# A decoder layer whose inputs are laid out by the host: one DMA for a token tile, contiguous weight tiles

## The chip, the cores and the metric

The kernel runs on one core of a Trainium2 chip. The time is that of the device for one launch, in microseconds (us). Rearranging arrays on the host before and after the launch is not in it. Before the change three runs gave 2838.21, 2841.0 and 2851.06 us, so the median is 2841.0 us.

The engines are PE (TensorE, matrix products), DVE (VectorE), ACT (ScalarE), POOL (GpSimd) and SP (SyncE). In this kernel SP issues every DMA, one after the other, and the 16 DMA engines of the core carry them out.

## The reference

One decoder layer on 2048 tokens of 1024 numbers, all in float32:

```python
h  = rmsnorm(x, g_mix)
zb, zc, zx, zq, zk, zv = split(h @ w_in)          # 6 x 512 columns
y_c = zb * causal_dwconv3(zc * zx, conv_w, conv_b)
y_a = dilated_attention(rmsnorm(zq), rmsnorm(zk), zv)   # 8 heads, 3 branches: dilation 1, 4, 16
x  = x + concat(rmsnorm(y_c, g_out_conv), rmsnorm(y_a, g_out_attn)) @ w_out
h  = rmsnorm(x, g_ffn)
x  = x + (silu(causal_dwconv3(h @ w_gate, ...)) * (h @ w_up)) @ w_down      # 2816 wide
x  = x + sigmoid(rmsnorm(x, g_ple) @ w_ple_gate) * (p @ w_ple_proj)
```

## The kernel before

A float32 product is made of three matmuls: each operand is split into a high and a low half (`split`, L91 and L92: ACT rounds, POOL or DVE subtracts), and `mm3` (L95) adds high x high, high x low and low x high. With an operand 512 wide one such matmul is the unit of PE's work here.

The 2048 tokens are four chunks `c` of 512. In a chunk the tokens are reordered, so that the dilated branches read plain slices: the token 16a + b of a chunk (a below 32, b below 16) stands at 32b + a. A tile of 128 rows therefore holds four values of b, with 32 tokens each. In the array x these 32 tokens lie 16 rows apart. `tokens` (L65 to L69) loads or stores such a tile as four DMAs of 32 partitions, one for each b. It is used for x at the start (tile `xt`), for x again in the first residual (tile `t` of `project`), for p in the last stage, and for the result.

The program has three parts in a row. `qkv` normalizes and transposes x, multiplies with the q, k and v columns of w_in and spills the results to DRAM. `mix` runs the attention and, paced beside it, the convolution group, whose weights come as tiles `craw` (L286). `rest` runs a list of stages: three `project` stages (w_out and the residual), `gate_up` and `down` for two halves of the tokens, and `ple`. Products of 2 x 2 blocks are made with seven block products instead of eight.

In `project` (its name stands in `rest`), chunks 0 and 1 are treated together, first the convolution's part of w_out in two halves of 512 columns. For each half and each chunk, a loop over four k blocks loads y (`load_y`, L823, tile `s`), splits it to a tile `g` on ACT (L828) and DVE (L829), and runs 12 matmuls on it. After a chunk DVE adds the result to x (L906, tile `t`), and the sum is stored to `xd` (L908). Tiles `s` and `g` have four buffers each, tiles `t` eight.

The order of the instructions on each engine is not that of the code. The framework's scheduler puts them in order with a model of their durations; then each engine, and SP's queue of DMAs too, runs in that fixed order. An instruction that waits holds up all behind it on its engine. The DMAs take turns on eight completion semaphores, and a DMA whose turn comes waits until the DMA eight places before it has landed, as the wait lists of the built program have it.

Of the kernel before, what the change touches and what calls it, by code (L numbers as in the profile page):

```python
# [19 lines left out]
P = 128  # L20
SEQ = 2048
D = 1024
DFF = 2816
PLE = 256
CW = 512
NH = 8
HD = 64
KD = D // P
# [11 lines left out]
class Layer:  # L40


    def __init__(self, tc, a, out, ctx):
        self.tc, self.nc, self.a, self.out, self.ctx = tc, tc.nc, a, out, ctx
        nc = self.nc
        self.const = ctx.enter_context(tc.tile_pool(reuse_waits="tile", name="const", bufs=1))
        self.dram = ctx.enter_context(tc.tile_pool(name="dram", bufs=1, space=DRAM))
        self.ident = self.const.tile([P, P], F32, name="ident")
        make_identity(nc, self.ident)
        d = self.dram  # L50
        self.hd = [d.tile([KD, P, QT], F32, name=f"hd{c}") for c in range(NQ)]
        self.qd = [d.tile([2, 2, HD, SEQ], F32, name=f"qd{p}") for p in range(4)]
        self.kd = [d.tile([2, 2, HD, SEQ], F32, name=f"kd{p}") for p in range(4)]
        self.vd = [d.tile([QT, NH, 2 * HD], F32, name=f"vd{c}") for c in range(NQ)]
        self.ycd = [d.tile([P, SEQ], F32, name=f"ycd{i}") for i in range(4)]
        self.yad = [d.tile([P, SEQ], F32, name=f"yad{i}") for i in range(4)]
        self.xd = [[[d.tile([P, D], F32, name=f"xd{i}{c}{j}") for j in range(4)] for c in range(NQ)] for i in range(3)]
        self.gd = [d.tile([7, NF // 2, P, QT], F32, name=f"gd{h}") for h in range(2)]
        self.bd = [[d.tile([P, D], F32, name=f"bd{i}{j}") for j in range(4)] for i in range(2)]
        self.td = [d.tile([NF // 2, P, 2, 512], F32, name=f"td{i}") for i in range(2)]  # L60
        self.xq = a["x"].rearrange("(c a b) m -> c b a m", a=32, b=16)
        self.pq = a["p"].rearrange("(c a b) m -> c b a m", a=32, b=16)
        self.oq = out.rearrange("(c a b) m -> c b a m", a=32, b=16)

    def tokens(self, tile, dram, c, j, store=False):  # L65

        for b in range(4):
            rows, part = dram[c, 4 * j + b], tile[32 * b:32 * b + 32]
            self.nc.sync.dma_start(*((rows, part) if store else (part, rows)))  # L69

    def rsqrt(self, pool, ss, n, scale):

# [56 lines left out]
    def qkv(self):  # L129
        nc, tc, a = self.nc, self.tc, self.a  # L130
        with ExitStack() as st:
# [11 lines left out]
            gq = wvp.tile([P, 4], F32, name="gq")  # L143

            def gains():
                for i in range(2):
                    nc.sync.dma_start(gk[64 * i:64 * i + 64], a["k_norm_g"].rearrange("(d o) -> d o", o=1))
                    nc.sync.dma_start(gq0[64 * i:64 * i + 64], a["q_norm_g"].rearrange("(d o) -> d o", o=1))
                for p in range(4):
                    for i in range(2):  # L150
                        s = slice(64 * i, 64 * i + 64)
                        nc.vector.tensor_scalar(gq[s, p:p + 1], gq0[s], 2.0 ** (2 * p + i - 2), None, ALU.mult)

            whl = {w: [(wvp if w == 2 else wp).tile([P, KD, 512], F32R, name=f"w{w}{s}") for s in "hl"] for w in range(3)}
            wv = a["w_in"].rearrange("(k p) n -> p k n", p=P)

            def load_w(w):
                for k in range(0, KD, 2):
                    raw = stage.tile([P, 2, 512], F32, name="raw", tag="raw")
                    c0 = 3 * CW + 512 * w  # L160
                    nc.sync.dma_start(raw, wv[:, k:k + 2, c0:c0 + 512])
                    self.split(whl[w][0][:, k:k + 2], whl[w][1][:, k:k + 2], raw, nc.gpsimd if w or k % 4 else nc.vector)

            def load_x(c, j):
# [114 lines left out]

    def load_conv_w(self, n):  # L280
        nc, pool = self.nc, self.cwp
        c0 = CW * (1, 2, 0)[n % 3] + P * (n // 3 % 4)
        halves = []
        for k in range(0, KD, 4):
            raw = pool.tile([P, 4, P], F32, name="craw", tag="craw", bufs=4)
            nc.sync.dma_start(raw, self.a["w_in"].rearrange("(k p) n -> p k n", p=P)[:, k:k + 4, c0:c0 + P])  # L286
            hi = pool.tile([P, 4, P], F32R, name="chi", tag="chi", bufs=5)
            lo = pool.tile([P, 4, P], F32R, name="clo", tag="clo", bufs=5)
            (nc.scalar.copy if k else nc.vector.tensor_copy)(hi, raw)  # L289
            nc.gpsimd.tensor_tensor(lo, raw, hi.bitcast(F32), ALU.subtract)  # L290
            halves.append((hi, lo))
        return [(hi[:, k], lo[:, k]) for hi, lo in halves for k in range(4)]

    def conv(self):

        nc, a, st = self.nc, self.a, self.cst
        cp = st.enter_context(self.tc.tile_pool(reuse_waits="tile", side="right", name="cp", bufs=1))
        work = st.enter_context(self.tc.tile_pool(reuse_waits="tile", side="right", name="cwork", bufs=1))
        cw = cp.tile([P, 4, 3], F32, name="cw")
        cb = cp.tile([P, 4], F32, name="cb")  # L300
        for i in range(3):
            nc.sync.dma_start(cw[:, :, i], a["conv_w"][i].rearrange("(k p) -> p k", p=P))
        nc.sync.dma_start(cb, a["conv_b"].rearrange("(k p) -> p k", p=P))
        carry = cp.tile([P, 4, 2, 2, 1], F32, name="carry")
        yield
        cols = [(c, i, z) for c in range(NQ) for i in range(4) for z in (1, 2, 0)]
        w, hq = self.conv_w, self.conv_h
        for n, (c, i, z) in enumerate(cols):
            if n and i == 0 and z == 1:
                hq = self.load_conv_h(c)  # L310
            ps = self.cpm.tile([P, QT], F32, name="zps", tag="zps")
            for k in range(KD):
                m = self.mm3(ps, *w[k], hq[k][:, 0], hq[k][:, 1], k == 0, k == KD - 1)
                if k % 2 == 0:
                    self.pace(m, 4 * n + k // 2)
            if n + 1 < len(cols):
                w = self.load_conv_w(n + 1)
            if z == 1:
# [12 lines left out]
            yield  # L331
# [260 lines left out]
    def weight_units(self, stages):  # L592
# [4 lines left out]
        for name, *arg in stages:  # L597
# [5 lines left out]
            elif name == "gate_up":  # L603
                for f in range(NF // 2):
                    for w in (a["w_gate"], a["w_up"]):
                        yield w.rearrange("(k p) n -> p k n", p=P)[:, :, 2 * f * P:2 * f * P + 2 * P]
            elif name == "down":
                b = a["w_down"].rearrange("(f i p) (s n) -> i s p f n", i=2, p=P, n=512)
                t = [t.rearrange("f p s n -> s p f n") for t in self.td]
                for m in (b[0, 0], t[1][1], b[1, 0], t[0][1], t[0][0], t[1][0], b[1, 1]):  # L610
                    for f in range(0, NF // 2, 2):
                        yield m[:, f:min(f + 2, NF // 2)]
# [40 lines left out]
    def rest(self):  # L653
# [3 lines left out]
        with ExitStack() as st:  # L657
# [16 lines left out]
            row = lambda tag: (rows if tag == "t" else sums if tag == "c" else small).tile([P, 512], F32, name=tag, tag=tag)  # L674
            operand = lambda tag="w": (big if tag == "w" else late).tile([P, 2, 512], F32R, name=tag, tag=tag)
            go = cp.tile([P, 2, 4], F32, name="go")
            for i, n in enumerate(("g_out_conv", "g_out_attn")):
                nc.sync.dma_start(go[:, i], a[n].rearrange("(k p) -> p k", p=P))
            cw = cp.tile([P, NF, 3], F32, name="fcw")
            cb = cp.tile([P, NF], F32, name="fcb")  # L680
            for i in range(3):
                nc.sync.dma_start(cw[:, :, i], a["ffn_conv_w"][i].rearrange("(k p) -> p k", p=P))
            nc.sync.dma_start(cb, a["ffn_conv_b"].rearrange("(k p) -> p k", p=P))
            carry = cp.tile([P, NF, 2, 1], F32, name="fcarry")
            ones = cp.tile([P, 1], F32, name="ones")
            nc.vector.memset(ones, 1.0)
# [496 lines left out]
    return r  # L1183


def build(shapes):
    nc = bacc.Bacc("TRN2", target_bir_lowering=False, num_devices=1, dynamic_dma_scratch_size=1024)
    a = {n: nc.dram_tensor(f"in_{n}_dram", s, F32, kind="ExternalInput").ap() for n, s in shapes.items()}
# [19 lines left out]
```

## Time and profile before

| | us |
|---|---|
| median of three runs | 2841.0 |
| the profiled execution | 2845.52 |
| its span, first to last instruction | 2843.8 |
| PE busy in the span | 2638.9 |
| DVE busy | 1908.9 |
| POOL busy | 1520.2 |
| ACT busy | 1320.3 |

The 16 DMA engines moved 467.66 MB of the kernel's data and were busy for 53.2% of the span. PE is busy for 93% of the span, so what is to be gained lies in the stretches in which PE waits. They are found in the table of busy time by 40 us, and the reason in the list of waits and in the order of events on each engine. The trace's mean clock of PE is 0.977 of the full one; the table names the clock for each stretch.

### The profile page before, as it was taken

The page shows a single profiled execution, that of the slowest core. Times are in us where ns is not written, and L with a number is a line of the kernel's source. Part 1 is how long each engine was busy: PE and PEld are TensorE (multiplying, and loading weights), DVE is VectorE, ACT ScalarE, POOL GpSimd, SP SyncE. Part 2 cuts the span into 40 slices and gives each one's busy share as a digit, 9 for nine tenths or more (in the row PEclk, how much of TensorE's full clock was granted, in tenths as well). Part 3 has the DMA queues.
Part 4 walks back from the last instruction along what each step waited for, and adds up shares of the span by engine and source line. Part 5 has one row for each costly group of instructions (what it writes and reads, how often), then busy time and mean ns, then how long its engine had stood idle before and what let it go on. Part 6 is the DMA issues. An engine that isn't in the chain of part 4 may idle for free. (4 is left out here: it accounts for less than half of the span.)

```text
span 2843.8 us, 38213 instructions
## 1 busy us (share of the span) xinstructions
PE 2638.9 (93%) x12320; PEld 2174.1 (76%) x12320; DVE 1908.9 (67%) x3355; ACT 1320.3 (46%) x2941; POOL 1520.2 (53%) x1050
## 2 busy tenths in 40 slices
PE   6999989999899869899889999999999999998998
PEld 5777778888788658677677787877878777786787
DVE  8776656767676555987767778457677776647543
ACT  3322257767768234453334444444444445444332
POOL 4111311624343724478786678575666668767554
PEclk9999989999899989999999999999999999999999
DMA  6444566675755778665552236673323326665343
GB/s 185 149 136 124 174 151 152 182 173 148 196 154 152 213 222 306 195 224 205 199 193 97 97 125 213 232 240 106 101 102 104 112 89 212 222 227 195 97 124 88
DMA packets 374473, 470.10 MB, mean 165 GB/s; under 512 B 51072, under 2 KB 214528, under 8 KB 374272
## 3 DMA queue, kind: packets, MB, share of 16 engines
q1 hardware_dynamic: 374272, 467.66, 53.2%
q8 instruction: 97, 1.59, 0.2%
q14 instruction: 104, 0.85, 0.1%
HBM read 339.53 MB, written 127.99 MB: 164 GB/s over the span
## 5 line engine op out<-in xcount | busy, mean ns | idle before, releaser
L95 PE MATMUL ps<-t,w 128*128 128x512 f32 x4368 | 1034.4, 396 | 45.9 <-DVE u L757 23.1
L95 PEld LDWEIGHTS ps<-t,w 128*128 128x128 f32 x4368 | 819.8, 189 | 247.2 <-DVE u L757 28.7
L92 POOL TENSOR_TENSOR w<-raw,w 128x512 fp32r<-128x512 f32 x318 | 477.3, 1510 | 298.4 <-ACT w L91 281.9
L92 POOL TENSOR_TENSOR w<-s,w 128x512 fp32r<-128x512 f32 x208 | 298.8, 1441 | 178.4 <-ACT w L91 172.4
L95 PE MATMUL ps<-w,g 128*128 128x512 f32 x1368 | 342.6, 399 | 52.9 <-ACT g L828 22.3
L95 PEld LDWEIGHTS ps<-w,g 128*128 128x128 f32 x1368 | 258.2, 191 | 118.8 <-ACT g L828 24.9
L290 POOL TENSOR_TENSOR clo<-craw,chi 128x512 fp32r<-128x512 f32 x96 | 125.8, 1317 | 394.7 <-ACT chi L289 132.1
L95 PE MATMUL zps<-hq,chi 128*128 128x512 f32 x768 | 257.1, 412 | 9.2 <-DVE yc L329 5.9
L91 ACT CAST w<-raw 128x512 fp32r<-128x512 f32 x318 | 192.5, 615 | 94.1 <-PE ps L95 90.8
L91 ACT CAST w<-s 128x512 fp32r<-128x512 f32 x208 | 127.9, 617 | 228.3 <-PE ps L95 196.2
L95 PE MATMUL ps<-w,t 128*128 128x512 f32 x852 | 212.1, 395 | 6.8 <-POOL w L92 4.7
L440 ACT ACTIVATE pt<-so,md 128x256 f32<-128x256 f32 (+1 forms) x384 | 174.9, 457 | 84.5 <-DVE md L437 82.6
L95 PEld LDWEIGHTS ps<-w,t 128*128 128x128 f32 x852 | 160.8, 190 | 44.8 <-POOL w L92 7.3
L437 DVE CUSTOM_DVE_ANT_0 so<-s,neg 128x256 f32<-128x256 f32 (+1 forms) x384 | 130.3, 362 | 64.8 <-PE s L434 53.1
L706 DVE TENSOR_TENSOR s<-raw 128x512 f32<-128x512 f32 x88 | 113.4, 1289 | 83.4 <-POOL w L92 82.5
L95 PEld LDWEIGHTS zps<-hq,chi 128*128 128x128 f32 x768 | 142.1, 196 | 35.2 <-DVE yc L329 7.2
L92 DVE TENSOR_TENSOR g<-g 128x512 fp32r<-128x512 f32 x84 | 97.2, 1162 | 98.2 <-ACT g L91 93.2
L95 PE MATMUL zps<-hq,clo 128*128 128x512 f32 x384 | 154.5, 403 | 0.0
L433 PE MATMUL s<-kk,qs 128*128 128x256 f32 (+1 forms) x384 | 132.9, 353 | 20.6 <-DMA kk<-kd 18.2
L434 PE MATMUL s<-kk,qs 128*128 128x256 f32 (+1 forms) x384 | 137.1, 361 | 14.8 <-DMA v<-vd 5.8
L174 POOL TENSOR_TENSOR raw<-hT 128x1024 f32<-128x1024 f32 x16 | 39.0, 2438 | 202.4 <-DVE rs_h L78 187.5
L473 DVE TENSOR_TENSOR nb<-po,nb 64x512 f32<-64x512 f32 x96 | 92.1, 959 | 63.9 <-ACT nb L472 62.9
(214 smaller groups left out, 5118.4 us busy)
## 6 DMA issues: line engine op xcount, KB each, us to landing
gd<-t SPq DMA_DIRECT2D x110, 256.0 KB, 2.0
craw<-in_w_in_dram SPq DMA_DIRECT2D x96, 256.0 KB, 4.0
raw<-in_w_gate_dram SPq DMA_DIRECT2D x44, 512.0 KB, 3.7
raw<-in_w_up_dram SPq DMA_DIRECT2D x44, 512.0 KB, 3.5
g<-gd SPq DMA_DIRECT2D x84, 256.0 KB, 4.3
raw<-td SPq DMA_DIRECT2D x40, 512.0 KB, 4.0
t<-gd SPq DMA_DIRECT2D x70, 256.0 KB, 4.3
v<-vd SPq DMA_DIRECT2D x264, 64.0 KB, 2.6
```

Source lines behind the costliest of these rows:

```text
L91: self.nc.scalar.copy(hi, src)
L92: lo_engine.tensor_tensor(lo, src, hi.bitcast(F32), ALU.subtract)
L95: mm = lambda *a, **k: self.nc.tensor.matmul(*a, **k, **kw)
L174: nc.gpsimd.tensor_tensor(t, hT[:, :, 0].bitcast(F32), hT[:, :, 1].bitcast(F32), ALU.add)
L290: nc.gpsimd.tensor_tensor(lo, raw, hi.bitcast(F32), ALU.subtract)
L433: mm(s[:, lo:], qb[l], cols[0], start=True, stop=False)
L434: mm(s[:, lo:], qb[l], cols[1], start=False, stop=True)
L437: nc.vector.tensor_tensor_reduce(out=so[:, lo:], in0=s[:, lo:], in1=neg[:, br, lo:], scale=-slope, scalar=3.0e38, op0=ALU.add, op1=ALU.min ...
L440: nc.scalar.activation(pt[:, l, lo:], so[:, lo:], AF.Exp, bias=md[:, 0, col:col + 1], scale=-1.0, accum_out=md[:, 1, col:col + 1])
L473: nc.vector.tensor_tensor(dst, like(po[other], br), dst, ALU.add)
L706: nc.vector.tensor_tensor(t, x, y, op)
```

## The change

The host now rearranges the inputs before the launch, and the result after it (`lay_out`, and the last line of `kernel`); it computes nothing. x, p and the result stand in the kernel's order of tokens, so a tile of 128 tokens is one DMA of 128 partitions. The columns of w_in for the convolution are cut into 12 tiles of 128 columns, those for q, k and v into three of 512, w_gate and w_up into tiles of 256 columns, each with the partition first, so that what a partition receives is contiguous. Filters, biases and gains are stored by partition as well, and each is one DMA.

```diff
-        self.xq = a["x"].rearrange("(c a b) m -> c b a m", a=32, b=16)
-        self.pq = a["p"].rearrange("(c a b) m -> c b a m", a=32, b=16)
-        self.oq = out.rearrange("(c a b) m -> c b a m", a=32, b=16)
+        self.xq, self.pq, self.oq = [t.rearrange("(c j r) m -> c j r m", c=NQ, r=P) for t in (a["x"], a["p"], out)]
 
     def tokens(self, tile, dram, c, j, store=False):
-        for b in range(4):
-            rows, part = dram[c, 4 * j + b], tile[32 * b:32 * b + 32]
-            self.nc.sync.dma_start(*((rows, part) if store else (part, rows)))
+        self.nc.sync.dma_start(*((dram[c, j], tile) if store else (tile, dram[c, j])))
...
-                for i in range(2):
-                    nc.sync.dma_start(gk[64 * i:64 * i + 64], a["k_norm_g"].rearrange("(d o) -> d o", o=1))
-                    nc.sync.dma_start(gq0[64 * i:64 * i + 64], a["q_norm_g"].rearrange("(d o) -> d o", o=1))
+                nc.sync.dma_start(gk, a["k_norm_g"])
+                nc.sync.dma_start(gq0, a["q_norm_g"])
...
-                    nc.sync.dma_start(raw, wv[:, k:k + 2, c0:c0 + 512])
+                    nc.sync.dma_start(raw, a["w_qkv"][w, :, k:k + 2])
...
-            nc.sync.dma_start(raw, self.a["w_in"].rearrange("(k p) n -> p k n", p=P)[:, k:k + 4, c0:c0 + P])
+            nc.sync.dma_start(raw, self.a["w_conv"][z, :, k:k + 4])
...
-        for i in range(3):
-            nc.sync.dma_start(cw[:, :, i], a["conv_w"][i].rearrange("(k p) -> p k", p=P))
-        nc.sync.dma_start(cb, a["conv_b"].rearrange("(k p) -> p k", p=P))
+        nc.sync.dma_start(cw, a["conv_w"])
+        nc.sync.dma_start(cb, a["conv_b"])
...
-                        yield w.rearrange("(k p) n -> p k n", p=P)[:, :, 2 * f * P:2 * f * P + 2 * P]
+                        yield w[f]
...
-            for i, n in enumerate(("g_out_conv", "g_out_attn")):
-                nc.sync.dma_start(go[:, i], a[n].rearrange("(k p) -> p k", p=P))
+            nc.sync.dma_start(go, a["g_out"])
...
+def lay_out(a):
+    by = lambda t, shape, *axes: np.ascontiguousarray(t.reshape(shape).transpose(axes))
+    tokens = lambda t: by(t, (NQ, 32, 16, -1), 0, 2, 1, 3).reshape(SEQ, -1)
+    w_in, g_out = a.pop("w_in"), np.stack([a.pop("g_out_conv"), a.pop("g_out_attn")])
+    return dict(
+        a, x=tokens(a["x"]), p=tokens(a["p"]), g_out=by(g_out, (2, 4, P), 2, 0, 1),
+        w_conv=by(w_in[:, :3 * CW], (KD, P, 12, P), 2, 1, 0, 3), w_qkv=by(w_in[:, 3 * CW:], (KD, P, 3, 512), 2, 1, 0, 3),
...
```

The scheduler gives the changed program another order in four places: the first tiles of x, the first loads of the convolution's weights, the `project` stages, and the stores of `ple`. Everywhere else each engine has the same order as before.

On SP, at the end of `mix` and the beginning of the first `project`, the order was this (`s` is the tile of y for a k block, `ycd` and `yad` the stored y of the two groups, `xd` the stored residual):

```order
L823 DMA s<-ycd_84 128x512
L330 DMA ycd_84<-yc 128x512
L69 DMA t<-in_x_dram 32x512 x18
L908 DMA xd_89<-t 128x512
L908 DMA xd_90<-t 128x512
L908 DMA xd_91<-t 128x512
L69 DMA t<-in_x_dram 32x512
L908 DMA xd_92<-t 128x512
L69 DMA t<-in_x_dram 32x512 x13
```

It goes on with four `e<-yad`, the stores `xd_93` to `xd_96` with three pieces of `t` between them, and 13 further pieces; only then comes the next `s<-ycd_81`. Now the same place reads:

```order
L813 DMA s<-ycd_84 128x512
L322 DMA ycd_84<-yc 128x512
L65 DMA t<-in_x_dram 128x512 x8
L813 DMA e<-yad_85 128x512
L813 DMA e<-yad_86 128x512
L813 DMA e<-yad_87 128x512
L813 DMA e<-yad_88 128x512
L813 DMA s<-ycd_81 128x512
L813 DMA s<-ycd_82 128x512
L813 DMA s<-ycd_83 128x512
L813 DMA e<-yad_85 128x512
L898 DMA xd_89<-t 128x512
```

Three of the four `s` tiles of the next half have moved ahead of every store of the residual; the fourth, `s<-ycd_84`, stands behind `xd_89` to `xd_92` and one load of `t`.

Later, where `project` for chunks 2 and 3 begins, SP's order was this (`s<-yad` is again the y of a k block):

```order
L823 DMA s<-yad_85 128x512
L69 DMA t<-in_x_dram 32x512 x32
L823 DMA s<-yad_86 128x512
L823 DMA s<-yad_87 128x512
L823 DMA s<-yad_88 128x512
```

And now:

```order
L813 DMA s<-yad_85 128x512
L65 DMA t<-in_x_dram 128x512
L813 DMA s<-yad_86 128x512
L65 DMA t<-in_x_dram 128x512 x4
L813 DMA s<-yad_87 128x512
L65 DMA t<-in_x_dram 128x512 x3
L813 DMA s<-yad_88 128x512
```

The loads of x no longer stand in one block ahead of the last three `s` tiles.

On DVE the first rows of the program were these, behind the normalization of the first tile (`rs_*` are the steps of a reciprocal root, `hn` is the normalized tile, `gq` the scaled gain of q):

```order
L113 SCALAR_TENSOR_TENSOR hn<-xt,rs_y,g_mix 128x1024
L92 TENSOR_TENSOR w0l<-raw,w0h 128x1024
L125 TENSOR_TENSOR hT<-tp,hT 128x4x128
L92 TENSOR_TENSOR w0l<-raw,w0h 128x1024
L152 TENSOR_SCALAR gq<-gq_171 64x1 x4
L125 TENSOR_TENSOR hT<-tp,hT 128x4x128
```

Now they are:

```order
L109 SCALAR_TENSOR_TENSOR hn<-xt,rs_y,g_mix 128x1024
L88 TENSOR_TENSOR w0l<-raw,w0h 128x1024 x2
L147 TENSOR_SCALAR gq<-gq_171 64x1
L121 TENSOR_TENSOR hT<-tp,hT 128x4x128
L147 TENSOR_SCALAR gq<-gq_171 64x1 x6
L121 TENSOR_TENSOR hT<-tp,hT 128x4x128
```

The low half of the first transposed tile, `hT`, now stands behind two splits of weights and one step on the gain.

## Rows read from the trace of the kernel before

**Rows 1.** The page, its first two rows.

```profile
span 2843.8 us, 38213 instructions
...
PE 2638.9 (93%) x12320; PEld 2174.1 (76%) x12320; DVE 1908.9 (67%) x3355; ACT 1320.3 (46%) x2941; POOL 1520.2 (53%) x1050
```

**Rows 2.** Busy us of PE, PEld, DVE, ACT, POOL; clock; DMA share; GB/s.

```profile
1000.00:1040.00 40.00, 21.90 (x105) 18.00 (x103) 18.49 (x44) 10.91 (x17) 9.80 (x7) 0.82 0.72 219
1040.00:1080.00 40.00, 35.66 (x145) 28.10 (x146) 22.53 (x31) 20.00 (x33) 18.18 (x13) 0.93 0.90 306
1080.00:1120.00 40.00, 40.00 (x177) 32.37 (x177) 18.29 (x37) 14.30 (x31) 17.94 (x14) 1.00 0.87 313
1120.00:1160.00 40.00, 33.45 (x152) 26.77 (x151) 34.20 (x69) 18.28 (x37) 13.48 (x8) 0.94 0.63 207
1160.00:1200.00 40.00, 36.68 (x173) 29.23 (x172) 34.32 (x63) 22.94 (x47) 11.87 (x9) 0.98 0.62 200
```

**Rows 3.** Timeline of PE: start, us, what, count, idle before and releaser.

```profile
1004.32 12.55 PE L95 MATMUL ps<-w,g 128*128 128x512 f32 x54
...
1040.11 14.04 PE L95 MATMUL ps<-w,g 128*128 128x512 f32 x48 [18.22 <-ACT g L828]
1057.07 3.02 PE L95 MATMUL ps<-w,g 128*128 128x512 f32 x12 [2.92 <-ACT g L828]
...
1062.69 8.46 PE L95 MATMUL ps<-w,g 128*128 128x512 f32 x36 [1.20 <-ACT g L828]
```

**Rows 4.** Timeline of ACT at the end of that wait.

```profile
1039.34 0.72 ACT L828 ACTIVATE g<-s,go 128x512 fp32r<-128x512 f32 x1 [6.48 <-DMA s<-ycd]
```

**Rows 5.** Timeline of SP's queue before that load.

```profile
1003.55 11.34 SPq L69 DMA_DIRECT2D t<-in_x_dram  x18
...
1017.61 6.02 SPq L69 DMA_DIRECT2D t<-in_x_dram  x13
1023.68 1.84 SPq L823 DMA_DIRECT2D e<-yad  x4
...
1030.08 5.90 SPq L69 DMA_DIRECT2D t<-in_x_dram  x13
1036.08 0.37 SPq L823 DMA_DIRECT2D s<-ycd  x1
```

**Rows 6.** Waits of PE, 1110 to 1260: total us, times, longest.

```profile
PE ps L95 <- DVE g L829: 5.4, 5, 3.0
```

**Rows 7.** Timelines of SP and DVE in that stretch.

```profile
1123.99 15.21 SPq L69 DMA_DIRECT2D t<-in_x_dram  x32
1139.31 1.32 SPq L823 DMA_DIRECT2D s<-yad  x3
...
1134.90 7.96 DVE L792 SCALAR_TENSOR_TENSOR e<-e,rs_y,gain 128x1024 f32<-128x1024 f32 x4
```

**Rows 8.** Waits of PE in the first 80 us.

```profile
PE tp L122 <- DVE hn L113: 10.9, 1, 10.9
PE ps L95 <- DVE hT L125: 4.7, 1, 4.7
...
PE ps L95 <- ACT w0h L91: 2.4, 1, 2.4
```

**Rows 9.** Waits of PE, 320 to 400, then 400 to 920.

```profile
PE s L433 <- DMA kk<-kd: 7.5, 2, 6.0
PE s L434 <- DMA kk<-kd: 4.3, 1, 4.3
...
PE s L433 <- DMA kk<-kd: 10.7, 5, 3.4
...
PE s L434 <- DMA v<-vd: 5.8, 3, 3.2
```

**Rows 10.** DMA issues: count, KB each, median us from issue to landing.

```profile
craw<-in_w_in_dram SPq DMA_DIRECT2D x96, 256.0 KB, 4.0
raw<-in_w_gate_dram SPq DMA_DIRECT2D x44, 512.0 KB, 3.7
...
g<-gd SPq DMA_DIRECT2D x84, 256.0 KB, 4.3
...
raw<-in_w_down_dram SPq DMA_DIRECT2D x30, 512.0 KB, 3.4
```

**Rows 11.** The end: SP's last issues, and the chain's last piece.

```profile
2829.13 12.23 SPq L69 DMA_DIRECT2D out_dram<-s  x16
...
2838.92 0.69 DVE s L1143
```

More of the change, by code (lines that the diff above doesn't have):

```diff
@@ L154, in qkv @@
             whl = {w: [(wvp if w == 2 else wp).tile([P, KD, 512], F32R, name=f"w{w}{s}") for s in "hl"] for w in range(3)}
-            wv = a["w_in"].rearrange("(k p) n -> p k n", p=P)
             def load_w(w):
@@ L159, in load_w @@
                     raw = stage.tile([P, 2, 512], F32, name="raw", tag="raw")
-                    c0 = 3 * CW + 512 * w
-                    nc.sync.dma_start(raw, wv[:, k:k + 2, c0:c0 + 512])
+                    nc.sync.dma_start(raw, a["w_qkv"][w, :, k:k + 2])
                     self.split(whl[w][0][:, k:k + 2], whl[w][1][:, k:k + 2], raw, nc.gpsimd if w or k % 4 else nc.vector)
@@ L281, in load_conv_w @@
         nc, pool = self.nc, self.cwp
-        c0 = CW * (1, 2, 0)[n % 3] + P * (n // 3 % 4)
+        z = 4 * (1, 2, 0)[n % 3] + n // 3 % 4
         halves = []
@@ L676, in rest @@
             go = cp.tile([P, 2, 4], F32, name="go")
-            for i, n in enumerate(("g_out_conv", "g_out_attn")):
-                nc.sync.dma_start(go[:, i], a[n].rearrange("(k p) -> p k", p=P))
+            nc.sync.dma_start(go, a["g_out"])
             cw = cp.tile([P, NF, 3], F32, name="fcw")
             cb = cp.tile([P, NF], F32, name="fcb")
-            for i in range(3):
-                nc.sync.dma_start(cw[:, :, i], a["ffn_conv_w"][i].rearrange("(k p) -> p k", p=P))
-            nc.sync.dma_start(cb, a["ffn_conv_b"].rearrange("(k p) -> p k", p=P))
+            nc.sync.dma_start(cw, a["ffn_conv_w"])
+            nc.sync.dma_start(cb, a["ffn_conv_b"])
             carry = cp.tile([P, NF, 2, 1], F32, name="fcarry")
@@ L1183, in steps @@
     return r
+def lay_out(a):
[5 more added lines that the diff above has]
+        w_conv=by(w_in[:, :3 * CW], (KD, P, 12, P), 2, 1, 0, 3), w_qkv=by(w_in[:, 3 * CW:], (KD, P, 3, 512), 2, 1, 0, 3),
+        conv_w=by(a["conv_w"], (3, 4, P), 2, 1, 0), conv_b=by(a["conv_b"], (4, P), 1, 0),
+        q_norm_g=np.tile(a["q_norm_g"], 2)[:, None], k_norm_g=np.tile(a["k_norm_g"], 2)[:, None],
+        w_gate=by(a["w_gate"], (KD, P, NF // 2, 2 * P), 2, 1, 0, 3), w_up=by(a["w_up"], (KD, P, NF // 2, 2 * P), 2, 1, 0, 3),
+        ffn_conv_w=by(a["ffn_conv_w"], (3, NF, P), 2, 1, 0), ffn_conv_b=by(a["ffn_conv_b"], (NF, P), 1, 0))
 def build(shapes):
@@ L1203 @@
     arrays = {n: np.ascontiguousarray(v[0]) for n, v in arrays.items()}
+    arrays = lay_out(arrays)
     arrays["steps"] = steps()
@@ L1206 @@
     r = run_bass_kernel_spmd(nc, [{f"in_{n}_dram": v for n, v in arrays.items()}], core_ids=[0])
-    return r.results[0]["out_0_dram"].reshape(1, SEQ, D)
+    return np.asarray(r.results[0]["out_0_dram"]).reshape(NQ, 16, 32, D).transpose(0, 2, 1, 3).reshape(1, SEQ, D)
```

## The prediction

> **What bounds the kernel now.** I read the page first: PE is busy for 2638.9 of 2843.8 us [rows 1], so the kernel is bound by PE, and a transfer is worth something only where PE waits for it. The table of busy time by 40 us then shows where PE is short. In its best stretches PE is busy for all 40 us; behind the start it is worst from 1000 to 1040, with 21.90 us, and 1120 to 1200 has 33.45 and 36.68 [rows 2].
>
> The timeline of PE names the hole: one wait of 18.22 us for the tile `g` that ACT's L828 makes, then 2.92 and 1.20 us for the same [rows 3]. ACT itself waited 6.48 us for `s<-ycd` [rows 4], and SP had issued that load at 1036.08 only [rows 5]. From 1003.55 until then SP was busy issuing without a pause of note, mostly `t<-in_x`, x in pieces of 32 partitions: 18, 13 and 13 pieces in 11.34, 6.02 and 5.90 us, and four in between. So this hole is neither PE's nor the DMA engines' (their share was 0.72, 219 GB/s [rows 2]): SP's queue is long, because a tile takes four issues, and the one load that PE needs stands at its end. The reader should see the same picture at 1123.99: 32 pieces in 15.21 us, and three `s<-yad` right behind them [rows 7].
>
> **The change part by part.**
>
> *The first `project`.* One issue costs 11.34/18 = 0.63 us at the dear end and 6.02/13 = 0.46 us at the cheap end [rows 5]; a whole 128-partition tile costs 1.84/4 = 0.46 us (`e<-yad` [rows 5]). The new order has 8 whole loads of `t` and 4 of `e` ahead of the first `s` of the second half: 12 x 0.46 = 5.5 us, so it is issued at about 1003.55 + 5.5 = 1009 instead of 1036. Landing, ACT and DVE took 1040.11 - 1036.08 = 4.0 us [rows 3, 5]; `g` is then there at 1013, and PE wants it at 1040.11 - 18.22 = 1021.9. The 18.22 us go, and so should 2.92 and 1.20, which are the same tile's later blocks. PE's clock adds to it: its 48 matmuls behind the wait took 14.04 us, while 54 before it took 12.55, 0.2324 each [rows 3]. 48 x 0.2324 = 11.2, so 2.9 us were lost to the lower clock after the idle time (the granted clock was 0.82 in the mean of that stretch [rows 2]). Together 18.22 + 2.92 + 1.20 + 2.9 = 25.2 us is the upper bound.
>
> What is late next? Two things. First `s<-ycd_84`, which now stands behind four stores that wait for DVE's L906. PE needs that fourth block 3 x 12 x 0.2324 = 8.4 us after 1021.9, at 1030; the stores of the first chunk can go when the first chunk is added up, which is before PE has finished the second chunk, before 1021.9. With the 4.0 us this is in time. Second, the traffic itself: the three stretches from 1000 to 1120 moved (219 + 306 + 313) x 40 us = 33.5 MB [rows 2]. At 313 GB/s, the fastest of the three, this takes 107 us, and only 13 of the 25 us could be saved; this is the lower bound. But PE lost nothing in the stretch with 313 GB/s, and the share there was 0.87, so 313/0.87 = 360 GB/s may be had, and 33.5 MB then take 93 us. I take 20 us, nearer to the upper end.
>
> *The second `project`, 1120 to 1200.* PE lost 6.55 + 3.32 = 9.9 us there [rows 2], of which 5.4 us wait for DVE's L829 [rows 6]. The `s<-yad` come up to 1139.31 - 1123.99 = 15 us earlier. But DVE was busy for 34.2 and 34.3 us of 40, and one L829 stood behind four L792 of 7.96 us [rows 7]; in the new order DVE has two of these four ahead of it. I take 3 us, between 0 and 6.
>
> *The start.* PE cannot begin before 10.9 us [rows 8]. One load of x saves three issues, 1.4 us, of which the loads of weights behind it profit; the wait of 2.4 us for `w0h` should go, and the third tile's wait of 4.7 us for `hT` should get shorter [rows 8], as the next tiles of x stand nearer to the front. Against this, the first `hT` on DVE now stands behind two splits and a step on the gain `gq`, whose load lies behind six large ones. DVE is the engine that is short here. I take 3 us; the bounds are -4 (the whole of that detour) and +9 (the 2.4, the 4.7 and 2 us of the first wait).
>
> *The begin of `mix`.* PE waits 7.5 + 4.3 us for `kk` [rows 9]. Before these loads SP and the DMA engines have three filters of 4-byte pieces fewer to serve; I take 2 us, from -2 (the convolution's loads now come earlier in the queue, ahead of what attention needs) to 6, half of the waits.
>
> *Longer pieces.* The `craw` tiles go from 512-byte to 2 KB pieces, w_gate and w_up from 1 KB to 4 KB. Yet `craw` landed in 4.0 us, and `g<-gd` of the same 256 KB, with 2 KB pieces, in 4.3; w_gate in 3.7, w_down with its 2 KB pieces in 3.4 [rows 10]. So 0.3 us in a load at most, and the loads are ahead of their use. During `mix` PE waits for DMA 10.7 + 5.8 us [rows 9]. I take 1 us, from 0 to 6.
>
> The Trainium skill (DMA: Bandwidth & Descriptors, section "Why small descriptors are slow (HBM only)") gives each packet a fixed overhead of about 3 cycles beside its beats of 32 bytes, which would make 512-byte pieces 19/16 against 67/64, so 13% dearer than 2 KB ones. By that rule a `craw` of 4.0 us would fall to 3.5; the rows above show no such difference for `craw`, and the sum goes by them.
>
> *The end.* The last result is computed at 2838.92 + 0.69 = 2839.6, and SP's last four issues end at 2841.36, of 16 [rows 11]. One issue instead of four at 0.46 saves about 1.1 us (0.8 to 1.6).
>
> Sum: 20 + 3 + 3 + 2 + 1 + 1.1 = 30 us. Against the profiled execution's own 2845.5 us this gives 2815.5; that execution was 4.5 us above the median of the runs, 2841.0, so on their scale the forecast is 2811. All lower bounds together (13 + 0 - 4 - 2 + 0 + 0.8 = 8) give 2833, all upper ones (25 + 6 + 9 + 6 + 6 + 1.6 = 54) give 2787.
>
> **The rivals.**
>
> *The hole moves.* SP's order is fixed, and now the stores of the residual are nearer to the loads. If `xd_92` goes out at 1025 rather than 1017, because DVE is later or the loads of x are not there, `s<-ycd_84` lands late, then the next chunk's tiles, and most of the 18 us come back as several waits for L828. For it: SP really runs without a pause here; against it: each of these loads has some 10 us of slack. Then the place gives 5 instead of 20, the second `project` 0, the start 2, the rest 2: 9 us, 2832. No change.
>
> *The length of the pieces counts.* If PE's waits for `kk` and `v` (11.8 + 16.5 us [rows 9]) come from the 512-byte loads of `craw` that stand ahead on the DMA engines, and half of them go, 14 us come on top: 2797. Against it are the equal landing times [rows 10].
>
> *The tiles crowd each other.* Before, SP's slow issue of small pieces let `s` land in about 3 us. Now eight tiles of 256 KB, 2 MB, are thrown at the engines at once, ahead of `s`. At 219 GB/s [rows 2] these are 9.6 us. If each of the eight `s` blocks of the second half had to wait behind such a heap, PE would get one in 9 us, while it uses one in 2.8 us: 8 x 6.3 = 50 us of waits, against 22 + 3 now removed. The kernel would be slower by 25, less 11 elsewhere: 2855. It decides from a landing time of `s` of about 6 us on, lasting over both chunks; only eight free buffers of `t` exist, so the heap comes once, which speaks against it.
>
> **How the numbers follow.** Forecast 0.69 (2811, its own range 2797 to 2825); the hole moves 0.19 (2832); the length counts 0.07 (2797); crowding 0.05 (2855). The range from 2793 to 2834 takes in the first three and most of the bounds. A measurement of this kernel tells 0.5%, 14 us, from no change. Faster than that, below 2826.8, are the forecast but for 0.03 of it, and the third: 0.73. Within it: 0.22. Slower: 0.05.
>
> **What would show it.** In the new profile the 40 us behind the first `project`'s begin should have PE at 37 us or more instead of 21.90, with a clock near 1.0; the first `s<-ycd` of the second half should be issued some 6 us behind the eighth load of `t`'s start, and no wait of PE for L828 should exceed 4 us. In the second `project` the waits for L829 should be shorter and DVE as busy as before. PE's waits for `kk` should stay about 28 us in all. It is wrong if PE's wait for L828 is still over 10 us in sum (the hole moved), if the landing of `s<-ycd` is above 6 us there (crowding), or if the gain lies in `mix` and `gate_up` (the pieces).

## The result and the profile after

The changed kernel took 2811.09 us, the median of four runs (2807.87 to 2815.15), against 2842.88 for the kernel before in the same comparison: a ratio of 0.9886 [0.9858, 0.9914]. The forecast was 2811. When both kernels were run again later, on one chip, the ratio was 0.986 [0.9841, 0.9879]: 2809.65 us against 2849.69. So the gain is 32 us by the first comparison and 40 by the second. All intervals are at 95%.

The profiled execution took 2808.71 us, with a span of 2806.9, so these two profiles lie 36.9 us apart. The first rows of the page after answer to [rows 1]:

```profile
span 2806.9 us, 37793 instructions
...
PE 2639.7 (94%) x12320; PEld 2177.8 (78%) x12320; DVE 1907.3 (68%) x3355; ACT 1318.3 (47%) x2941; POOL 1523.5 (54%) x1050
```

In sum PE is as busy as before, to 0.8 us, so in this pair of profiles what the change gave is time in which PE waited. When both kernels were profiled again, PE was busy for 2642.8 us before and 2634.2 after, so there 8.6 us of the gain are busy time. Behind the first 40 us, in which PE is busy for 23.91 us (18.84 before), the table of busy time, in the columns of [rows 2], has no stretch like the one of 21.90 us any more. The first `project` now begins at 979.17, so the second row below, which starts 4 us behind that, answers to the first of [rows 2]:

```profile
0.00:40.00 40.00, 23.91 (x94) 18.18 (x95) 29.65 (x76) 17.96 (x27) 16.85 (x13) 0.96 0.67 221
...
983.20:1023.20 40.00, 34.46 (x148) 27.62 (x149) 29.06 (x53) 17.79 (x30) 13.41 (x9) 0.96 0.85 276
...
1000.00:1040.00 40.00, 35.10 (x156) 28.11 (x155) 34.17 (x46) 22.87 (x39) 25.55 (x18) 1.00 0.91 296
1040.00:1080.00 40.00, 40.00 (x181) 32.55 (x180) 19.86 (x42) 15.18 (x33) 19.38 (x15) 1.00 0.99 354
```

The timeline of PE shows the same place. [Rows 3] had a wait of 18.22 us there for ACT's `g`, and then 48 matmuls at a lower clock:

```profile
991.15 12.55 PE L91 MATMUL ps<-w,g 128*128 128x512 f32 x54
...
1004.35 6.65 PE L91 MATMUL ps<-w,g 128*128 128x512 f32 x28
1012.56 1.67 PE L91 MATMUL ps<-w,g 128*128 128x512 f32 x6 [1.56 <-DVE g L819]
1015.22 1.65 PE L91 MATMUL ps<-w,g 128*128 128x512 f32 x6 [0.99 <-DVE g L819]
1019.23 17.08 PE L91 MATMUL ps<-w,g 128*128 128x512 f32 x74 [2.35 <-DVE t L896]
```

No wait for ACT's L818 (L828 before) is left in this stage. What is late next is DVE, with three waits of 4.90 us in all; at the beginning of the stage PE waits 3.42 us more for DVE's `yc` (1.80 before). The 74 matmuls behind these waits took 0.231 us each, in a stretch whose granted clock was 1.00, the upper of its two levels. Why the wait for ACT is gone, SP's queue shows, in the columns of [rows 5]:

```profile
979.90 3.63 SPq L813 DMA_DIRECT2D s<-ycd  x4
...
984.18 4.57 SPq L65 DMA_DIRECT2D t<-in_x_dram  x8
988.80 3.67 SPq L813 DMA_DIRECT2D e<-yad  x4
992.90 3.17 SPq L813 DMA_DIRECT2D s<-ycd  x3
```

The first `s` of the second half goes out 8.7 us behind the start of the loads of `t`. In [rows 5] it was 1036.08 - 1003.55 = 32.5 us.

Split by stage (each begins with the first matmul on its tiles in the timeline of PE; two profiles of each kernel, the second pair from the later runs). "First `project`" is all of `project` for chunks 0 and 1, the convolution's part and the attention's; "second `project`" is that for chunks 2 and 3:

| stage, us | before | after | mean gain | forecast |
|---|---|---|---|---|
| start to the convolution's first product | 333.7, 333.2 | 328.5, 327.9 | 5.3 | 3 |
| from there to the first product with `kk` | 27.5, 28.4 | 25.0, 25.8 | 2.6 | 2 |
| from there to the first `project` | 634.8, 628.7 | 625.6, 626.0 | 6.0 | 1 |
| first `project` | 120.4, 124.0 | 103.7, 102.2 | 19.2 | 20 |
| second `project` | 115.6, 117.4 | 115.3, 115.3 | 1.2 | 3 |
| `gate_up` to the end | 1611.9, 1609.1 | 1608.7, 1609.8 | 1.2 | 1.1 |
| span | 2843.8, 2840.8 | 2806.9, 2806.9 | 35.4 | 30 |

In the first `project` PE was idle for 24.2 and 24.5 us before and for 8.4 and 6.9 after. The rest of what that stage gained, 0.8 and 4.2 us, is busy time, at a granted clock of 0.91 and 0.89 before and 0.98 after. Between single profiles the last stage, which has the same matmuls in all 14, took from 1608.6 to 1618.5 us, so a few us in one profile prove nothing there.

### The profile page after: what moved, and what is told of

It reads as the page before. It is cut to its first block, busy times and chain, and to the rows that moved or that the text cites. A ratio compares the mean times of both kernels' runs of the same rounds, so it can differ in the third digit from the quotient of the medians.

```text
span 2806.9 us, 37793 instructions
## 1 busy us (share of the span) xinstructions
PE 2639.7 (94%) x12320; PEld 2177.8 (78%) x12320; DVE 1907.3 (68%) x3355; ACT 1318.3 (47%) x2941; POOL 1523.5 (54%) x1050
## 3 DMA queue, kind: packets, MB, share of 16 engines
q1 hardware_dynamic: 283664, 467.64, 52.4%
## 5 line engine op out<-in xcount | busy, mean ns | idle before, releaser
L91 PE MATMUL ps<-w,g 128*128 128x512 f32 x1368 | 344.3, 401 | 33.4 <-POOL w L88 14.5
L425 PE MATMUL s<-kk,qs 128*128 128x256 f32 (+1 forms) x384 | 133.2, 353 | 16.3 <-DMA kk<-kd 14.5
```

The costliest lines, as they stand in the source:

```text
L91: mm = lambda *a, **k: self.nc.tensor.matmul(*a, **k, **kw)
L425: mm(s[:, lo:], qb[l], cols[0], start=True, stop=False)
```

## The experiments

Ratios are to the kernel before, run on the same chip in the same comparison.

### One half of the change at a time

**The token tiles alone:** `tokens`, and x, p and the result in the kernel's order; weights, filters and gains as before.

```diff
+        self.xq, self.pq, self.oq = [t.rearrange("(c j r) m -> c j r m", c=NQ, r=P) for t in (a["x"], a["p"], out)]
...
-        for b in range(4):
-            rows, part = dram[c, 4 * j + b], tile[32 * b:32 * b + 32]
-            self.nc.sync.dma_start(*((rows, part) if store else (part, rows)))
+        self.nc.sync.dma_start(*((dram[c, j], tile) if store else (tile, dram[c, j])))
```

> Only x, p and the result are laid out by the host; weights and filters are read as before. Theory A (SP's issues of token tiles made the hole): the wait of PE for L828's tile at the first project falls from 22 us to under 5, the stretch from the first product with w_out to the first with the second part shrinks by about 18 us, the start by about 5, and the kernel takes 23 to 27 us less than before (ratio 0.990 to 0.992). Theory B (the length of the pieces of weights matters): the 9 us that the attention and convolution stage lost stay lost here, so the lead of about 16 us with which the changed kernel comes to its first project is only 5 to 7 us here. Rival (the order that the scheduler made, or the run's own scatter, gave the 9 us in the mix): that lead is over 12 us here as well.

0.9928 [0.9904, 0.9951], 2827.14 us, a little less gain than the 0.990 to 0.992 expected. The start took 329.0 us and the first `project` 105.2, almost what the whole change gives there; the waits for ACT's `g` are 1.8 us in all. `mix` (from the first product with `kk` to the first `project`) took 636.4. The kernel came to its first `project` 2.0 us sooner than before; theory B had 5 to 7, the rival over 12.

**Everything but the token tiles,** which stay four DMAs in the old layout:

```diff
+                    nc.sync.dma_start(raw, a["w_qkv"][w, :, k:k + 2])
...
+            nc.sync.dma_start(raw, self.a["w_conv"][z, :, k:k + 4])
...
+                        yield w[f]
...
+            nc.sync.dma_start(fcw, a["ffn_conv_w"])
```

> The other half of the change: weights and filters by partition, x, p and the result as before in four pieces a tile. Theory A: the hole at the first project stays, 15 us or more in PE's wait for L828, and what is gained is 3 us or so from the filters there. Theory B: the attention and convolution stage gains 6 to 10 us, so the kernel takes 8 to 13 us less than before (ratio 0.995 to 0.997). Rival (scatter): ratio 0.998 to 1.0.

0.9956 [0.9939, 0.9973], 2837.27 us. The hole stays; these are the rows of PE's timeline:

```profile
1030.02 13.70 PE L95 MATMUL ps<-w,g 128*128 128x512 f32 x48 [14.09 <-ACT g L822]
1045.89 3.02 PE L95 MATMUL ps<-w,g 128*128 128x512 f32 x12 [2.17 <-ACT g L822]
```

0.9928 x 0.9956 = 0.9884, so the two halves add up to the whole change. The token tiles are worth 20 us (14 to 27 by the interval) and the rest 12.5 (8 to 17). The forecast had given that rest some 3 us.

**The convolution's weights alone, and the filters and gains alone:**

```diff
+            nc.sync.dma_start(raw, self.a["w_conv"][z, :, k:k + 4])      # weights alone
...
+            nc.sync.dma_start(go, a["g_out"])                            # filters and gains alone
+            nc.sync.dma_start(fcw, a["ffn_conv_w"])
```

> Only the convolution's weights are laid out in tiles (2 KB pieces instead of 512 B), and the order of all engines is that of the kernel before. Theory B: 5 to 9 us less than before, all between 330 and 996 us, with PE's waits for kk and v falling from 28 us to about 20. Rival (the pieces don't matter): within 3 us of before, waits for kk and v at 26 to 30 us.

> Only the filters, biases and gains are stored by partition, one DMA each; each engine has the same order as in the kernel with all but the token tiles. Theory A: SP's 7 us for six filter DMAs ahead of the first project become 1.5, but the 48 pieces of x still stand behind, so PE's wait for L828 falls by 5 us at most; with 1 us from the begin of the mix the kernel takes 2 to 7 us less (ratio 0.9975 to 0.999). If the tiny pieces block the DMA engines for the attention's first loads, the begin of the mix (PE's waits for kk up to 400 us) gains 3 us or more.

0.9981 [0.9965, 0.9997] and 0.9965 [0.995, 0.9981]; the filters gave more than the 2 to 7 us expected, 10 us (5 to 14 by the interval). Two things follow. The loads of `craw` land somewhat sooner when their pieces go from 512 bytes to 2 KB. [Rows 10] had 4.0 us; these are the rows of the run with the new weights alone, and of the changed kernel:

```profile
craw<-in_w_conv_dram SPq DMA_DIRECT2D x96, 256.0 KB, 3.5
...
craw<-in_w_conv_dram SPq DMA_DIRECT2D x96, 256.0 KB, 3.9
```

One pair of profiles would not show it, but all of them do: the five with the old layout have medians of 4.0 to 4.7 us, the seven with the new one whose loads are on SP's queue 3.3 to 3.9. It does not reach PE's waits for `kk` and `v`. They were 25.4 us with the new weights alone (28.3 before), where theory B wanted 20, and over all these profiles 26.2 to 31.8 us with the old layout and 25.1 to 32.6 with the new one.

The filters, which I had costed at the begin of `mix` only, also stand in front of the first `project`. These are SP's rows there, of the kernel before and then of the one with new filters only:

```profile
991.58 0.43 SPq L678 DMA_DIRECT2D go<-in_g_out_conv_dram  x1
...
992.67 3.94 SPq L682 DMA_DIRECT2D fcw<-in_ffn_conv_w_dram  x3
996.66 1.84 SPq L683 DMA_DIRECT2D fcb<-in_ffn_conv_b_dram  x1
998.60 1.58 SPq L823 DMA_DIRECT2D s<-ycd  x1
```

```profile
982.94 0.42 SPq L675 DMA_DIRECT2D go<-in_g_out_dram  x1
983.42 0.45 SPq L678 DMA_DIRECT2D fcw<-in_ffn_conv_w_dram  x1
983.91 0.43 SPq L679 DMA_DIRECT2D fcb<-in_ffn_conv_b_dram  x1
...
987.12 3.63 SPq L819 DMA_DIRECT2D s<-ycd  x4
```

Three filters of 4-byte pieces hold the queue for 3.94 us and the one new load for 0.45; the first `s` comes 4.2 us behind `go` instead of 7.0. The hole follows. Its longest wait is 18.22 us before, 17.72 when run again and 18.95 with the convolution's weights alone; it is 14.00 with the filters alone and 14.09 in the run above. So about 4 us of the hole belonged to the filters. The stage as a whole took 121.4 us with the filters alone, though, against 120.4 and 124.0 before, so how much of it reached the time is not shown.

### The number of pieces, with the new layout

In the changed kernel x is loaded in four or two pieces a tile again, in `project` or at the start. Everything else keeps the new layout, so the pieces now lie side by side in DRAM.

```diff
+        for s in [slice(P // pieces * i, P // pieces * (i + 1)) for i in range(pieces)]:
+            self.nc.sync.dma_start(*((dram[c, j][s], tile[s]) if store else (tile[s], dram[c, j][s])))
...
-                                        self.tokens(x, self.xq[..., cols], c, j)
+                                        self.tokens(x, self.xq[..., cols], c, j, pieces=4)     # or 2
...
-                self.tokens(xt, self.xq, c, j)
+                self.tokens(xt, self.xq, c, j, pieces=4)                                       # the run at the start
```

> The changed kernel with the new layout throughout, but x in `project` is again issued as four pieces of 32 partitions a tile; they now lie side by side in DRAM, and each is as long as before. Theory A (the number of issues in SP's queue makes the hole): the 36 or so pieces stand ahead of the first `s<-ycd` of the second half again, at 0.46 to 0.63 us each, so PE's longest wait for ACT's `g` (L818) in the first `project` is 10 us or more again, the time from the first product of the first `project` to the first of the second is 115 to 122 us instead of 104, and the kernel's time is 0.994 to 0.996 of the kernel before (the changed kernel: 0.989). Theory B (the layout in DRAM counts, rows that lie 16 apart against rows side by side): no long wait, 104 us, 0.989.

0.9943 [0.9928, 0.9957], as theory A had it. The first `project` takes 120.6 us again. SP's queue and PE's timeline have the old picture:

```profile
985.36 10.53 SPq L65 DMA_DIRECT2D t<-in_x_dram  x20
...
1000.59 4.64 SPq L65 DMA_DIRECT2D t<-in_x_dram  x10
...
1014.52 4.14 SPq L65 DMA_DIRECT2D t<-in_x_dram  x9
1018.76 0.37 SPq L813 DMA_DIRECT2D s<-ycd  x1
```

```profile
1023.68 13.79 PE L91 MATMUL ps<-w,g 128*128 128x512 f32 x48 [13.84 <-ACT g L818]
1040.49 5.49 PE L91 MATMUL ps<-w,g 128*128 128x512 f32 x12 [3.02 <-ACT g L818]
```

The rows' distance in DRAM is not what counts, since they are neighbours here. What counts is the number of issues, with one reservation: the order goes with it. In the runs with pieces the scheduler again has stores of `xd` ahead of that `s`, and no run has the pieces in SP's queue without them. An estimate separates the two. Ahead of the `s` the durations of the issues of `t` add up to 20.8 us here (48 of them) and to 3.7 in the changed kernel (8). Without these 17.1 us the `s` would have gone out 16.3 us behind the first `t` instead of 33.4, which by the slack found below leaves no wait. So the issues alone are enough for the hole.

> The changed kernel, but x in `project` is issued as two pieces of 64 partitions a tile. Theory A: some 24 issues of about 0.5 us stand ahead of the first `s<-ycd` of the second half, 12 us; it is issued at about 12 us behind the first of them, landing and splitting take 4 more, and PE wants it 18 us behind: no long wait yet, 2 us at most, so the stage takes 104 to 110 us and the ratio to the kernel before is 0.989 to 0.991. If the price grew in proportion to the issues (no slack), a third of the 17 us would come back, 110 us and 0.991 to 0.992.

0.9917 [0.9901, 0.9933], which is the range of the price in proportion. But the stage took 118.2 us, more than either theory had and almost as much as with four pieces (103.7 with one). I had expected slack to swallow the dose, and it did not:

```profile
984.41 10.38 SPq L65 DMA_DIRECT2D t<-in_x_dram  x15
...
1001.50 7.05 SPq L65 DMA_DIRECT2D t<-in_x_dram  x8
1008.65 0.53 SPq L813 DMA_DIRECT2D s<-ycd  x1
```

```profile
1015.24 2.08 PE L91 MATMUL ps<-w,g 128*128 128x512 f32 x4 [6.35 <-ACT g L818]
...
1076.94 20.78 PE L91 MATMUL ps<-w,t 128*128 128x512 f32 x76 [3.82 <-DVE t L896]
```

An issue of 64 partitions took 10.38/15 = 0.69 us and 7.05/8 = 0.88 with what stands between the issues (the median of one is 0.59), not the 0.5 assumed, and four stores and four `e` lie between. The load went out 24.2 us behind the first piece, not 12, and a wait of 6.35 us is left. That wait is less than half of the 14.5 us by which the stage grew. PE was idle for 15.8 us in it (8.4 with one piece), which takes in waits for DVE's `t`, 3.82 us of them in the last row. And it was busy for 102.3 us instead of 95.4 with the same matmuls, at a granted clock of 0.90 instead of 0.98: the 76 matmuls of that row took 0.273 us each. Over the doses the delay of that `s` behind the first `t` is 33.4 us with four pieces, 24.2 with two and 8.7 with one; the longest wait is 13.8, 6.35 and none. The delay less the wait is 19.6 and 17.9 us: about so much slack the place has before PE waits for that `s`.

> The changed kernel, but x at the start (`xt`) is issued as four pieces of 32 partitions. Theory A: the 5 us gained up to the first product of the convolution (328.5 us instead of 333.7) come back, nothing else does; PE's first transposes come at 10.9 us instead of 9.3; the `project` stages stay at 104 us; ratio 0.990 to 0.991. Rival (the 5 us come from the gains, which are two loads instead of four 4-byte ones): 328 to 330 us stays.

0.9904 [0.9884, 0.9923]. The first transposes come at 10.96 us (9.26 after the change), the convolution's first product at 334.4 (328.5), and the first `project` takes 104.1 us. The gain at the start is the number of issues too, not the gains' loads; with the filters and gains alone the convolution's first product came at 334.4 us as well.

### The old pieces from another queue

The kernel before, with the pieces of x in `project` issued by POOL:

```diff
-            self.nc.sync.dma_start(*((rows, part) if store else (part, rows)))
+            (q or self.nc.sync).dma_start(*((rows, part) if store else (part, rows)))     # q=nc.gpsimd in project
```

> The kernel before, old layout and four pieces a tile, but the pieces of x in `project` are issued by POOL's queue instead of SP's. Theory A (SP's queue is the hole): SP gets to the first `s<-ycd` of the second half after 4 loads of `e`, PE's waits for ACT's `g` (L828) fall from 22 us to under 4, and the stage takes 104 to 112 us instead of 120; the ratio is 0.993 to 0.997 unless POOL's issues hold up its subtractions, for which PE would then wait. Theory B (short strided pieces on the DMA engines make the loads late): the hole stays, 115 us or more.

1.0165 [1.0147, 1.0183]: slower by 47 us. As theory A had it, the wait for ACT's `g` is gone (1.0 us in the first `project`). But POOL also runs in a fixed order, and this is what it does there:

```profile
1014.26 0.98 POOL L69 DMA_DIRECT2D t<-in_x_dram  x2 [0.63 <-DMA t<-in_x_dram]
1039.83 1.29 POOL L92 TENSOR_TENSOR w<-raw,w 128x512 fp32r<-128x512 f32 x1 [24.59 <-ACT w L91]
1041.07 0.51 POOL L69 DMA_DIRECT2D t<-in_x_dram  x1
```

The remaining loads of `t` stand behind a subtraction that waits 24.59 us for ACT. Up to 1230 us PE then waits 22.2 us for DVE's L906, which needs `t`. The first `project` takes 139.9 us, not the 104 to 112 of theory A, and the second 140.7 (115.6 before). So the run shows that SP's queue made the wait for `g`, but not what the kernel would take with that queue free. Of the two in-order queues that took the pieces, both paid for them. The Trainium skill (Trainium Kernel Development and Optimization, section "Key Constraints") says that issuing from several engines only saves issue time. Here issue time was what was short, and the trace agrees, at 0.50 us an issue on POOL, but the place in the other queue cost more.

### Both kernels again, and an attempt at more

> The kernel before, unchanged, once more: it shows how far two profiles of one kernel differ by stage. Between the first product with `kk` and the first of the first `project`, the profiled executions so far took 634.8, 636.4 and 638.3 us where both the convolution's weights and the filters had the old layout, and 624.0 to 625.7 us where at least one of them had the new one. If the nine us are the layout's, this run takes 633 to 639 us there; if they are scatter of the clock from one execution to the next, it is as likely to take 624 to 630. The first `project` should take 119 to 121 us up to the second, as in the first profile, and the ratio is 0.998 to 1.002.

> The changed kernel, unchanged, once more: ratio 0.986 to 0.991; up to the first product of the convolution 328 to 330 us, the first `project` 103 to 105 us; between the first product with `kk` and the first `project` 623 to 627 us if the nine us there are the layout's, and anything up to 636 us if they are scatter.

1.0002 [0.9987, 1.0017] and 0.986 [0.9841, 0.9879]; the stages are in the table. `mix` took 628.7 us here, below the 633 that the layout theory wanted, so part of the nine us is the difference between executions. The first `project` took 124.0, above the 119 to 121 expected; with the convolution's weights alone, where `mix` is short too, it took 124.7, so with the old tiles the hole seems to take back part of what `mix` gains. Yet in eight profiles with new filters or weights for the convolution (all but the two that follow) it took 624.0 to 626.0, and in the four without either 628.7 to 638.3.

The last two try to take PE's remaining waits for `kk` and `v`: six buffers for `craw`, or its loads on POOL.

```diff
-            raw = pool.tile([P, 4, P], F32, name="craw", tag="craw", bufs=4)
+            raw = pool.tile([P, 4, P], F32, name="craw", tag="craw", bufs=6)             # the one
-            nc.sync.dma_start(raw, self.a["w_conv"][z, :, k:k + 4])
+            nc.gpsimd.dma_start(raw, self.a["w_conv"][z, :, k:k + 4])                    # the other
```

> The changed kernel with six buffers for the convolution's raw weights `craw` instead of four, which is no part of the change: an attempt at the 27 us for which PE still waits for `kk` and `v` in `mix`. In the profile of the changed kernel SP stands 54.6 us in `mix` before loads of `craw`, until POOL has read an older one, and the loads of `kk` and `v` stand behind them in the same queue. If that is what makes them late, the waits for `kk` and `v` fall to 15 us or less, `mix` takes 612 to 620 us, and the ratio is 0.982 to 0.986. Rival: `kk` is a single tile and its loads wait for PE's own reading; then the waits stay at 25 us or more and the ratio is that of the changed kernel, 0.987 to 0.990.

> The changed kernel, but the loads of `craw` are issued by POOL, which is the engine that frees their buffers; SP's queue then has none of them. If the loads of `kk` and `v` are late because they stand behind `craw` in SP's queue, PE's waits for them fall to 15 us or less. Against it POOL spends 0.5 us on each issue, as in the run with POOL's queue, and stands still where a load of `craw` has to wait; its `clo` and `ya` come later. The two together: ratio 0.984 to 0.992. If `kk` waits for PE's reading, nothing is won and the ratio is 0.989 to 0.995.

0.9914 [0.9897, 0.9932] and 0.9997 [0.9983, 1.0012]: both slower than the changed kernel. With six buffers SP still waits for POOL's `clo` 41.8 us (54.6 after the change), and its loads of `qs` wait 19.5 us for PE's reading of the old one, 8.9 after the change; `mix` takes 630.2 us. PE's waits for `kk` and `v` do fall, to 18.5 us from 29.5, between theory and rival. But waits for which the trace names no releaser, which the changed kernel has none of there, come to 11.8 us, so that PE's waits from 320 us on are 52.9 us in all as against 52.8. With POOL's queue `mix` takes 661.3, PE's waits for `kk` and `v` stay at 30.0, and it waits 14.1 us for DVE's `chi`. So neither run wins anything by getting `craw` out of the way of `kk`; whether it makes them late stays open. The changed kernel stays the fastest of all that ran.

## Why the prediction was right

*The first `project`* was sized at 20 us and gave 16.6 and 21.8 in the two pairs. The mechanism, SP's queue with too many issues, is shown from both ends: with the layout and four pieces the hole is back, and with the old layout and no pieces in SP's queue the wait for `g` is gone. Some details were off. The first `s` goes out after 8.7 us instead of 5.5, because a whole tile's issue took 4.57/8 = 0.57 us and one of `e` 3.67/4 = 0.92, not the 0.46 of [rows 5]. DVE keeps 4.9 us of the hole, where I had named `s<-ycd_84` and the traffic as next. PE was busy for 34.46 us of the 40, at a granted clock of 0.96, not 37 or more. Some 4 of the 18.22 us were the filters', which the step had not counted. And the clock, put at 2.9 us, gave 0.8 and 4.2.

The bound from the traffic came true in its upper reading: the engines moved 354 GB/s from 1040 to 1080 with PE at 40.00 us, near the 360 that I had estimated from [rows 2].

*The second `project`* was sized at 3 us and gave 0.3 and 2.1. The last three `s<-yad` did come earlier, from 8.0 us behind the stage's begin on instead of 23.0, but PE's waits for L819 are 5.5 us there, against 5.4 in [rows 6]. DVE was as busy as before, for 33.69 us from 1086.60 to 1126.60, the stretch that answers to the 34.20 us from 1120 to 1160. The earlier loads took nothing off the waits for it, so this step was wrong in kind, not only in size.

*The start* was sized at 3 us and gave 5.3; the run with four pieces there gave 5.8 back. The three saved issues bring PE's first matmul forward from 10.91 to 9.26 us, and the `hT` detour that I had feared costs two short waits of 0.85 and 1.20 us. The wait for `w0h` is gone, as forecast; PE's waits up to 80 us fall from 24.5 to 18.6 us in all.

*The begin of `mix`* was sized at 2 us and gave 2.6. With the filters alone this stretch is 26.4 us, with the convolution's weights alone 28.6, so it is the filters, as supposed.

*Longer pieces* were sized at 1 us, from the reading that the landing times would not change. They did change a little: `craw` lands in a median of 3.3 to 3.9 us instead of 4.0 to 4.7, w_gate in 3.6 to 3.7 instead of 3.7 to 4.0. By the Trainium skill's rule on short descriptors (DMA: Bandwidth & Descriptors, "Why small descriptors are slow (HBM only)") a `craw` of 4.0 us would have fallen to 3.5, by estimate. The traces agree: the mean of the medians is 4.3 us in the five old profiles and 3.8 in the seven new ones. But PE's waits for `kk` and `v` from 320 on are 29.5 us, against 28.3 in [rows 9], so the rival of the lengths falls.

`mix` behind its begin gave 9.2 and 2.7 us, and this is the step that failed: the sum had 1 us there, for the longer pieces. It is short in every profile in which the filters or the convolution's weights are new, with either alone, and no shorter with both. Two things go with it. PE's waits for which the trace names no releaser are 4.8 to 6.5 us in the four profiles without either and 0 to 2.5 in the eight. Before the change nearly all of them stood at the scores `s`, the product that reads `kk`. This is their row in PE's waits from 400 to 920 ("issue" stands for no releaser); after the change there is none like it:

```profile
PE s L434 <- issue: 4.7, 3, 2.3
```

And at an equal number of matmuls PE was busy for 583.9 us of it before and 577.1 after; from the 1200th to the 1650th of them the granted clock was 0.92 before and 0.98 after. The second pair does not repeat that, with 579.6 us before and 580.8 after. In the mean of the four profiles without new filters or weights PE is busy for 583.9 us and idle for 50.7, in that of the eight with them for 579.3 and 45.6. Why filters or weights should do this is open.

*The end* was sized at 1.1 us. SP's last issue now ends 0.36 us behind the last result instead of 1.75, as meant:

```profile
2792.51 10.84 SPq L65 DMA_DIRECT2D out_dram<-s  x4
```

The span, however, ends 3.55 us behind that row's end, and before, at 2843.75, 2.39 us behind the last of [rows 11]. So 1.2 of the 1.4 us that issuing saves are lost again and 0.2 are left. That the last, larger store lands later is likely, but its landing is not in the trace.

Of the rivals, the hole did not move. The tiles do crowd, without a price: the sign of it, a landing of `s<-ycd` above 6 us, came true, with 6.70 and 6.61 us for the first two of the second half. Two before the change had taken 6.52 and 6.74, so the 3 us that the rival started from held for the first at most. But the first now goes out at 992.90 and has landed at 999.6, and PE comes to it, by estimate, at 1008.5, 18 matmuls of 0.2324 us behind 1004.35; it did not wait for ACT.

That the total came out at 2811 owes something to luck: the token tiles gave 20 us where the steps had some 27, the upper end of their interval, and the rest 12.5 where they had 3. The kernel before, too, was measured at 2842.88 us in the first comparison and at 2849.69 in the later one, where the gain was 40 us and not 30.

## What to carry to other kernels

When one queue issues every DMA, count the issues ahead of the load that is late: a piece of 32 partitions cost as much as a tile of 128, and a layout that makes one DMA of four removes a hole that neither bandwidth nor packet length explains. A hole also costs more than its wait: over the first `project` PE's granted clock was 0.89 to 0.91 with it, and 0.98 in both profiles of the changed kernel. Look for the small loads too; six loads of filters and gains in 4-byte pieces in front of a stage were worth about 4 us of its longest wait. Before moving the pieces to another engine's queue, see what waits in that queue: here a subtraction did, for 24.59 us, and the loads behind it with it. And profile a kernel twice before explaining a few us of one stage: the clock of `mix` told a story in one pair that the other did not repeat.

## What the runs showed of the hardware

- An issue's time does not follow its size. On SP the median issue of `t` took 0.42 us for 32 partitions (64 KB, the kernel before), 0.59 for 64 and 0.38 for 128 (256 KB, the changed kernel); on POOL one took 0.50 for 32.
- Pieces of 4 bytes cost the queue more: 3.94/3 = 1.31 us for an `fcw` of 11 KB against 0.45 us for all 33 KB laid out by partition.
- 24% fewer packets for the same 467.6 MB took 2.8% off the DMA engines' busy time (53.2% of 2843.8 us, then 52.4% of 2806.9).
- A load of 256 KB in pieces of 2 KB landed some 12% sooner than in pieces of 512 bytes: medians of 3.3 to 3.9 us against 4.0 to 4.7.
